# Moving the four PSUM accumulators of the first two output-projection row tiles to the other bank set

## The chip, the cores and the metric

The kernel runs on one NeuronCore of one Trainium2 chip. The metric is the device time of one execution in microseconds (us), given as the median of several runs.

## What is computed

Two independent sequences of 512 rows and 1024 columns pass through a trunk of two layers. Cut to what matters here, one layer is:

```
h      = x @ w_in                                   # attention, HGRN2 and gate inputs
o_att  = window_attention(...)                      # 512 columns
o_hg   = hgrn2_branch(...)                          # 512 columns
mixed  = sigmoid(ga) * (o_att @ w_proj_att) + sigmoid(gb) * (o_hg @ w_proj_hgrn)
x      = layer_norm(ALPHA * x + mixed @ w_out)      # the output projection
x      = layer_norm(ALPHA * x + square(relu(x @ w_ff1)) @ w_ff2)
```

## The kernel before, in words

All values are fp32. Large matmuls are made of three passes: every operand is split into a high part (a cast to fp32r, on ACT) and a low part (the difference, on DVE or POOL), and `high*high + low*high + high*low` is accumulated in PSUM. The 1024 rows of both sequences stand as eight row tiles of 128; `g` is the sequence, `j` the row tile (0 to 7).

PSUM is one pool of two sets of four banks. `mm_ps` (line 109) hands out the four banks tagged `mm` in turn, `sm_ps` (line 112) the four tagged `sm`. An allocation of a set takes the bank that was given out four allocations earlier, and the first matmul into it waits until that bank's last reader is done. The framework sets these waits as semaphores. `mm` serves the projections; `sm` serves the transposes, the attention scores and values, the small products of HGRN2 and part of the second feed-forward matmul.

The stretch around the change, once per layer:

- **Branch projections** (lines 821 to 842). For each of eight column tiles `m_` and both sequences, `project` (line 190) runs 12 matmuls (lines 152 to 154) into an `mm` bank. In the second half of the loop (the attention branch), DVE reads the bank with the gate (line 838), adds the other branch (839), ACT casts the high part of `mixed` (841) and DVE subtracts for the low part (842). Line 838 is the only reader of the bank. The results are the tiles `mx`, 128 columns of `mixed` per step `k`.
- **Weights of the output projection** (`load_rows`, line 844, called in line 864). Eight row blocks `wo[0]` to `wo[7]` of `w_out` are loaded into the three buffers `raw`, cast on ACT (line 131) and subtracted on DVE (even blocks) or POOL (odd blocks) (line 132).
- **Output projection** (lines 871 to 904). `out_proj(j, n, k)` adds step `k` of row tile `j` and column half `n`: three matmuls (lines 879, 880, 881) of 128x512. The first `lead = 2` row tiles are done together with `k` outermost, so that four accumulators are open at once and each `wo[k]` is used for 12 matmuls as it arrives. Row tiles 2 to 7 follow one after the other, 24 matmuls per accumulator. DVE reads each accumulator in line 896 and goes on with the layer norm.
- **Transposes** `x1.put` (line 173). From `j = 4` on, the finished row tiles are transposed on PE into `sm` banks (line 180) and split by ACT (185) and DVE (186) for the first feed-forward matmul.

Each engine works its instructions off in the program's order; loads are issued by SP in the program's order.

Of the kernel before, what the change touches and what calls it, by code (L numbers as in the profile page):

```python
# [87 lines left out]
def tile_encoder_trunk(  # L88
# [20 lines left out]
    def mm_ps():  # L109
        return psum.tile([P, 512], F32, tag="mm", name="mm")  # L110
# [680 lines left out]
    for l in range(DEPTH):  # L791
# [20 lines left out]
        with tc.tile_pool(name=f"ff{l}", bufs=1) as fp:  # L812
# [55 lines left out]
            lead = 2  # L868
            pend = {}

            def out_proj(j, n, k):
                if k == 0:
                    pend[j, n] = mm_ps()
                g, r = divmod(j, 4)
                ts = slice(r * P, (r + 1) * P)
                h = slice(n * 512, (n + 1) * 512)
                mh, ml = mx.at(g, k, 0)[:, ts], mx.at(g, k, 1)[:, ts]
                wh, wl = wo[k][:, 0, h], wo[k][:, 1, h]
                nc.tensor.matmul(pend[j, n], mh, wh, start=(k == 0), stop=False)  # L879
                nc.tensor.matmul(pend[j, n], ml, wh, start=False, stop=False)  # L880
                nc.tensor.matmul(pend[j, n], mh, wl, start=False, stop=(k == KT - 1))  # L881

            for j in range(8):
                y = acc_tile()
                nc.sync.dma_start(y, x_rows(l, j))
                if j == 0:
                    for k in range(KT):
                        for i in range(lead):
                            for n in range(2):
                                out_proj(i, n, k)  # L890
                for n in range(2):
                    h = slice(n * 512, (n + 1) * 512)
                    if j >= lead:
                        for k in range(KT):
                            out_proj(j, n, k)
                    nc.vector.scalar_tensor_tensor(
                        y[:, h], y[:, h], ALPHA, pend.pop((j, n)), op0=ALU.mult, op1=ALU.add
                    )
                layer_norm(y, gb, fp)
                acc.append(y)  # L900
                if j >= 4:
                    x1.put(j - 4, acc[j - 4])
# [210 lines left out]
```

## Time and profile before

| | us |
|---|---|
| median of 3 runs | 3051.74 |
| lowest and highest of them | 3050.33, 3055.02 |
| the profiled execution, its own time | 3051.14 |
| its span in the trace | 3049.3 |
| PE busy | 2950.1 (97% of the span) |
| DVE busy | 1668.9 (55%) |
| ACT busy | 1092.6 (36%) |
| POOL busy | 862.1 (28%) |

The mean granted clock of TensorE is 0.989 of full speed over the span. The output projection of the first layer begins at 750.47 us, that of the second at 2261.03 us of the span. In the timeline, each row is one instruction or a few merged ones: its start, its length, the engine, the line in the kernel, what it writes from what, and in brackets how long the engine sat idle before it and what released it. Matmuls are pipelined, so that the next one starts before the length shown is over; the distance of their starts is what counts.

### The profile page before, as it was taken

The page shows a single profiled execution, that of the slowest core. Times are in us where ns is not written, and L with a number is a line of the kernel's source. Part 1 is how long each engine was busy: PE and PEld are TensorE (multiplying, and loading weights), DVE is VectorE, ACT ScalarE, POOL GpSimd, SP SyncE. Part 2 cuts the span into 40 slices and gives each one's busy share as a digit, 9 for nine tenths or more (in the row PEclk, how much of TensorE's full clock was granted, in tenths as well). Part 3 has the DMA queues.
Part 4 walks back from the last instruction along what each step waited for, and adds up shares of the span by engine and source line. Part 5 has one row for each costly group of instructions (what it writes and reads, how often), then busy time and mean ns, then how long its engine had stood idle before and what let it go on. Part 6 is the DMA issues. An engine that isn't in the chain of part 4 may idle for free.

```text
span 3049.3 us, 42766 instructions
## 1 busy us (share of the span) xinstructions
PE 2950.1 (97%) x16720; PEld 2398.4 (79%) x16720; DVE 1668.9 (55%) x2909; ACT 1092.6 (36%) x1858; POOL 862.1 (28%) x532
## 2 busy tenths in 40 slices
PE   8999999999999999999999999999999999989997
PEld 6777787877888887788777777878878888878886
DVE  5888748126444344445678887570265434344457
ACT  3344447422122222343333444473231222224332
POOL 4221111112222222454542221101131222234544
PEclk9999999999999999999999999999999999999999
DMA  3111222246123446533521112222470243564334
GB/s 127 36 40 39 67 83 68 82 160 212 48 84 132 160 161 244 193 97 111 168 76 36 43 43 70 84 67 98 160 227 6 102 154 138 188 254 159 96 118 146
DMA packets 278379, 348.77 MB, mean 114 GB/s; under 512 B 16033, under 2 KB 184609, under 8 KB 269985
## 3 DMA queue, kind: packets, MB, share of 16 engines
q1 hardware_dynamic: 276880, 342.82, 33.7%
q8 instruction: 132, 2.16, 0.3%
q10 hardware_dynamic: 1296, 3.21, 0.3%
q14 instruction: 71, 0.57, 0.1%
HBM read 238.77 MB, written 100.66 MB: 111 GB/s over the span
## 4 chain that ended last, share of the span: by engine, by line
PE 82%; DVE 11%; DMA 3%; issue 2%; ACT 1%; POOL 1%; SPq 0%; POOLq 0%; ACTq 0%; DVEq 0%
PE mm L152 17%; PE mm L154 16%; PE mm L153 16%; PE mm L978 3%; PE mm L979 3%; PE sm L978 3%; PE sm L979 3%; PE sm L980 3%; PE mm L980 3%; PE mm L879 2%; PE mm L881 2%; PE mm L880 2%; PE sm L709 1%; PE sm L655 1%; PE sm L699 1%
## 5 line engine op out<-in xcount | busy, mean ns | idle before, releaser
L152 PE MATMUL mm<-X,w 128*128 128x512 f32 x2624 | 1033.5, 394 | 3.2 <-ACT w L131 2.8
L153 PE MATMUL mm<-X,w 128*128 128x512 f32 x2624 | 1029.0, 392 | 1.1 <-DVE X L186 1.1
L154 PE MATMUL mm<-X,w 128*128 128x512 f32 x2624 | 1026.8, 391 | 1.0 <-POOL w L132 1.0
L132 POOL TENSOR_TENSOR w<-raw,w 128x1024 fp32r<-128x1024 f32 (+1 forms) x179 | 417.8, 2335 | 1362.9 <-ACT w L131 1238.7
L152 PEld LDWEIGHTS mm<-X,w 128*128 128x128 f32 x2624 | 493.7, 188 | 111.0 <-issue 3.8
L154 PEld LDWEIGHTS mm<-X,w 128*128 128x128 f32 x2624 | 494.1, 188 | 101.9 <-POOL w L132 1.9
L153 PEld LDWEIGHTS mm<-X,w 128*128 128x128 f32 x2624 | 494.1, 188 | 99.6 <-DVE X L186 1.4
L131 ACT CAST w<-raw 128x1024 fp32r<-128x1024 f32 (+1 forms) x330 | 321.2, 975 | 374.9 <-PE sm L980 106.6
L919 DVE TENSOR_TENSOR X<-t 128x512 f32<-128x512 f32 x128 | 88.5, 692 | 390.2 <-ACT t L918 390.2
L132 DVE TENSOR_TENSOR w<-raw,w 128x1024 fp32r<-128x1024 f32 (+1 forms) x153 | 184.4, 1210 | 174.3 <-ACT w L131 174.2
L968 POOL TENSOR_TENSOR raw<-X 128x512 f32<-128x512 f32 x128 | 173.7, 1359 | 227.9 <-DVE w L132 226.2
L918 ACT ACTIVATE t<-mm 128x512 f32<-128x512 f32 x128 | 76.5, 598 | 422.7 <-PE mm L154 422.7
L978 PE MATMUL mm<-w 128*128 128x512 f32 x480 | 190.1, 397 | 25.1 <-ACT w L131 19.3
L979 PE MATMUL mm<-w 128*128 128x512 f32 x480 | 189.6, 395 | 0.6 <-DVE w L132 0.6
L980 PE MATMUL mm<-w 128*128 128x512 f32 x480 | 189.0, 394 | 0.0
L978 PE MATMUL sm<-w 128*128 128x512 f32 x384 | 149.5, 389 | 0.0
L980 PE MATMUL sm<-w 128*128 128x512 f32 x384 | 149.4, 389 | 0.0
L979 PE MATMUL sm<-w 128*128 128x512 f32 x384 | 149.4, 389 | 0.0
L978 PEld LDWEIGHTS mm<-w 128*128 128x128 f32 x480 | 91.3, 191 | 46.6 <-ACT w L131 20.2
L808 DVE TENSOR_TENSOR X<-raw,X 128x512 fp32r<-128x512 f32 x32 | 20.7, 689 | 195.8 <-ACT X L807 195.8
L879 PE MATMUL mm<-X 128*128 128x512 f32 x256 | 102.9, 402 | 11.9 <-DVE t L838 11.9
L966 POOL TENSOR_TENSOR w<-X,w 128x512 fp32r<-128x512 f32 x64 | 85.0, 1329 | 97.6 <-ACT w L962 96.0
(190 smaller groups left out, 3918.1 us busy)
## 6 DMA issues: line engine op xcount, KB each, us to landing
hsp<-X SPq DMA_DIRECT2D x64, 1024.0 KB
raw<-hsp SPq DMA_DIRECT2D x192, 256.0 KB
raw<-in_w_in_dram SPq DMA_DIRECT2D x84, 512.0 KB
raw<-in_w_ff_dram SPq DMA_DIRECT2D x64, 512.0 KB
X<-in_w_ff_dram SPq DMA_DIRECT2D x32, 1024.0 KB
gates<-gt SPq DMA_DIRECT2D x64, 256.0 KB
t<-gates SPq DMA_DIRECT2D x64, 256.0 KB
w<-hsp SPq DMA_DIRECT2D x24, 512.0 KB
```

What stands on the lines that cost most here:

```text
L131: (first or nc.scalar.copy)(hi, src)
L132: (eng or nc.gpsimd).tensor_tensor(lo, src, hi.bitcast(F32), op=ALU.subtract)
L152: nc.tensor.matmul(ps, ah, bh, start=(i == 0), stop=False)
L153: nc.tensor.matmul(ps, ah, bl, start=False, stop=False)
L154: nc.tensor.matmul(ps, al, bh, start=False, stop=(i == n - 1))
L879: nc.tensor.matmul(pend[j, n], mh, wh, start=(k == 0), stop=False)
L919: nc.vector.tensor_tensor(out[g], t, t, op=ALU.mult)
L966: nc.gpsimd.tensor_tensor(w[:, 1, 512:], src, w[:, 0, 512:].bitcast(F32), op=ALU.subtract)
L968: nc.gpsimd.tensor_tensor(raw[:, 512:], block(b0, k), block(b1, k), op=op)
L978: nc.tensor.matmul(ps[r], hh, wh, start=first, stop=False, **kw)
L979: nc.tensor.matmul(ps[r], hh, wl, start=False, stop=False, **kw)
L980: nc.tensor.matmul(ps[r], hl, wh, start=False, stop=stop, **kw)
```

## The change

The four accumulators of the first two row tiles (`j < lead`, both halves `n`) are taken from the `sm` set; those of row tiles 2 to 7 come from `mm` as before. Nothing else differs.

```
 
             def out_proj(j, n, k):
                 if k == 0:
-                    pend[j, n] = mm_ps()
+                    pend[j, n] = (sm_ps if j < lead else mm_ps)()
                 g, r = divmod(j, 4)
```

The order of the instructions is the same on every engine; the tiles that they name and the semaphores that they wait for differ. The following rows stand on PE at the start of the output projection in the first layer, before the change (names with numbers are buffers: `mm_...` is an accumulator, the first `X_...` is `wo[0]`, the second is the high or low part of `mixed`; in brackets the semaphores by the engine or queue that raises them).

```order
L154 MATMUL mm_6912<-X_6225,w_6888 128x512
L879 MATMUL mm_6987<-X_6931,X_6283 128x512 [waits DMAHW4_49,DMAHW3_49,DMAHW5_49,DMAHW2_49,DMAHW6_49,DMAHW1_49,DMAHW7_49,DMAHW0_49,DVE_49]
L880 MATMUL mm_6987<-X_6931,X_6284 128x512
L881 MATMUL mm_6987<-X_6931,X_6283 128x512
L879 MATMUL mm_6991<-X_6931,X_6283 128x512 [waits DVE_49]
L880 MATMUL mm_6991<-X_6931,X_6284 128x512
L881 MATMUL mm_6991<-X_6931,X_6283 128x512
L879 MATMUL mm_6995<-X_6931,X_6283 128x512 [waits DVE_49]
L880 MATMUL mm_6995<-X_6931,X_6284 128x512
L881 MATMUL mm_6995<-X_6931,X_6283 128x512
L879 MATMUL mm_6999<-X_6931,X_6283 128x512 [waits DVE_49]
```

The same rows with the change:

```order
L154 MATMUL mm_6912<-X_6225,w_6888 128x512
L879 MATMUL sm_6987<-X_6931,X_6283 128x512 [waits DMAHW4_49,DMAHW3_49,DMAHW5_49,DMAHW2_49,DMAHW6_49,DMAHW1_49,DMAHW7_49,DMAHW0_49,PE_49]
L880 MATMUL sm_6987<-X_6931,X_6284 128x512
L881 MATMUL sm_6987<-X_6931,X_6283 128x512
L879 MATMUL sm_6991<-X_6931,X_6283 128x512
L880 MATMUL sm_6991<-X_6931,X_6284 128x512
L881 MATMUL sm_6991<-X_6931,X_6283 128x512
L879 MATMUL sm_6995<-X_6931,X_6283 128x512
L880 MATMUL sm_6995<-X_6931,X_6284 128x512
L881 MATMUL sm_6995<-X_6931,X_6283 128x512
L879 MATMUL sm_6999<-X_6931,X_6283 128x512
```

The wait for DVE is gone from all four first matmuls, and the first of them now waits for PE's own semaphore. Also gone is the wait for DVE at the first matmul of each of the next four accumulators (row tiles 2 and 3).

One wait appears that was not written out before, at step `k = 4` of the first accumulator, here with the change (`X_6951` is `wo[4]`; before, the row of line 881 had no brackets):

```order
L879 MATMUL sm_6999<-X_6946,X_6283 128x512
L880 MATMUL sm_6999<-X_6946,X_6284 128x512
L881 MATMUL sm_6999<-X_6946,X_6283 128x512
L879 MATMUL sm_6987<-X_6951,X_6285 128x512 [waits Activation_49]
L880 MATMUL sm_6987<-X_6951,X_6286 128x512
L881 MATMUL sm_6987<-X_6951,X_6285 128x512 [waits DVE_49]
L879 MATMUL sm_6991<-X_6951,X_6285 128x512
```

It is the wait for the low part of `wo[4]`, which DVE makes. Before, the DVE wait of an earlier row already covered it.

## Rows read from the trace of the kernel before

**Rows 1.** The page, part 1: busy time of each engine.

```profile
PE 2950.1 (97%) x16720; PEld 2398.4 (79%) x16720; DVE 1668.9 (55%) x2909; ACT 1092.6 (36%) x1858; POOL 862.1 (28%) x532
```

**Rows 2.** PE's waits: engine, line, for whom; us, times, longest.

```profile
PE mm L879 <- DVE t L838: 11.9, 6, 3.5
```

**Rows 3.** Timeline of PE, end of the projections and start of line 879, first layer.

```profile
727.80 0.39 PE L154 MATMUL mm<-X,w 128*128 128x512 f32 x1
...
750.24 0.39 PE L154 MATMUL mm<-X,w 128*128 128x512 f32 x1
750.47 0.39 PE L879 MATMUL mm<-X 128*128 128x512 f32 x1
...
752.30 0.50 PE L879 MATMUL mm<-X 128*128 128x512 f32 x1 [0.99 <-DVE t L838]
...
755.00 0.50 PE L879 MATMUL mm<-X 128*128 128x512 f32 x1 [1.74 <-DVE t L838]
...
759.48 0.80 PE L879 MATMUL mm<-X 128*128 128x512 f32 x1 [3.52 <-DVE t L838]
...
760.50 0.63 PE L881 MATMUL mm<-X 128*128 128x512 f32 x1
...
762.21 0.63 PE L879 MATMUL mm<-X 128*128 128x512 f32 x1
...
763.87 0.39 PE L879 MATMUL mm<-X 128*128 128x512 f32 x1
```

**Rows 4.** Timeline of PE, the same place in the second layer.

```profile
2261.03 0.39 PE L879 MATMUL mm<-X 128*128 128x512 f32 x1
...
2262.89 0.50 PE L879 MATMUL mm<-X 128*128 128x512 f32 x1 [1.02 <-DVE t L838]
...
2265.59 0.80 PE L879 MATMUL mm<-X 128*128 128x512 f32 x1 [1.74 <-DVE t L838]
...
2266.61 0.63 PE L881 MATMUL mm<-X 128*128 128x512 f32 x1
2270.08 0.80 PE L879 MATMUL mm<-X 128*128 128x512 f32 x1 [2.85 <-DVE t L838]
...
2275.16 0.39 PE L879 MATMUL mm<-X 128*128 128x512 f32 x1
```

**Rows 5.** Timeline of DVE in the same stretch, first layer.

```profile
751.56 0.68 DVE L838 TENSOR_TENSOR t<-mm,t 128x512 f32<-128x512 f32 x1
...
754.26 0.68 DVE L838 TENSOR_TENSOR t<-mm,t 128x512 f32<-128x512 f32 x1
754.86 1.22 DVE L132 TENSOR_TENSOR X<-raw,X 128x1024 fp32r<-128x1024 f32 x1
...
758.75 0.68 DVE L838 TENSOR_TENSOR t<-mm,t 128x512 f32<-128x512 f32 x1
759.35 1.21 DVE L132 TENSOR_TENSOR X<-raw,X 128x1024 fp32r<-128x1024 f32 x1
...
779.06 1.37 DVE L896 SCALAR_TENSOR_TENSOR acc<-acc,mm 128x512 f32<-128x512 f32 x2 [15.92 <-PE mm L881]
```

**Rows 6.** Windows around the waits: us, busy us (x instructions) by engine; PEclk, DMA share, GB/s.

```profile
750.40:763.00 12.60, 6.34 (x20) 4.17 (x19) 10.65 (x12) 5.79 (x8) 2.69 (x1) 0.73 0.94 309
...
2261.00:2275.00 14.00, 8.40 (x22) 5.56 (x21) 10.79 (x12) 6.16 (x8) 3.66 (x2) 0.63 0.96 298
```

**Rows 7.** Tile `sm` from 600 to 830 us, matmuls: ns min/median/max, first and last start.

```profile
L180 PE MATMUL sm<-ident,acc x16: 270/272/273, 813.5 to 826.1; 128*128 128x128 f32 x16
```

**Rows 8.** Timeline of POOL: the low part of `wo[7]`, first and second layer.

```profile
763.44 2.40 POOL L132 TENSOR_TENSOR X<-raw,X 128x1024 fp32r<-128x1024 f32 x1 [5.16 <-ACT X L131]
...
2274.03 2.39 POOL L132 TENSOR_TENSOR X<-raw,X 128x1024 fp32r<-128x1024 f32 x1 [5.16 <-ACT X L131]
```

**Rows 9.** The chain that ended last: the spilled-hidden read after the first feed-forward matmul.

```profile
1214.82 10.59 DMA raw<-hsp
...
2726.22 7.88 DMA raw<-hsp
```

More of the change, by code (lines that the diff above doesn't have):

```diff
@@ L872, in out_proj @@
                 if k == 0:
-                    pend[j, n] = mm_ps()
+                    pend[j, n] = (sm_ps if j < lead else mm_ps)()
                 g, r = divmod(j, 4)
```

## The prediction
> **What bounds the kernel now.** I read the page's busy times first: PE works for 97% of the span [rows 1], so a change pays only if it closes a gap on PE, or makes PE's instructions run quicker. Next came the list of PE's waits. Line 879, the first matmul of an accumulator, waits 11.9 us in all, in six pieces, and always for DVE's line 838 [rows 2]. That is the gate multiply that reads the bank of a branch projection.
>
> The timeline of PE shows where the six pieces lie: three at the start of each layer's output projection [rows 3, 4]. Since a wait for several things is put down to one of them, I checked the name against DVE's own timeline. Line 838 ends at 751.56 + 0.68 = 752.24, 754.26 + 0.68 = 754.94 and 758.75 + 0.68 = 759.43 us [rows 5]; PE starts again at 752.30, 755.00 and 759.48 [rows 3]. Each restart follows its release by about 0.06 us, so the bank really is what was missing. DVE comes late because between the gate multiplies it also makes the low parts of `wo` [rows 5]; PE has finished the projections by 750.47 and meets DVE's arrears.
>
> **What the waits cost.** The idle figures alone understate it, so I count start to start. Undisturbed, PE needs (750.24 - 727.80) / 99 = 0.2267 us per matmul (99 steps lie between these two rows) [rows 3]. In the first layer the matmul at 763.87 is the 22nd of the output projection, 21 steps after the one at 750.47. Undisturbed it would start at 750.47 + 21 x 0.2267 = 755.23, so 8.64 us are lost. In the second layer the 22nd starts at 2275.16 and would start at 2261.03 + 4.76 = 2265.79: 9.37 us are lost [rows 4]. Together 18.01 us.
>
> This splits in two. The holes themselves are the idle time in brackets plus what pipelining would have saved, 0.39 - 0.23 = 0.16 us each (0.63 - 0.23 = 0.40 for the last one of the second layer, which follows a 0.63 us matmul): 0.99 + 1.74 + 3.52 + 0.48 = 6.73 and 1.02 + 1.74 + 2.85 + 0.72 = 6.33 us, 13.1 together [rows 3, 4]. The other 4.9 us are slow matmuls. From 760.50 to 762.21, four steps take 0.427 us each, nearly twice the normal step [rows 3]; the granted clock over the two stretches is 0.73 and 0.63 on average [rows 6]. That is a mixture of the two levels, 2.4 and 1.2 GHz: after its holes PE runs at the lower one for a while.
>
> The Trainium skill, "TensorE: Matmul & The Clock Gate", section "A second HAM failure mode: psum-queue depth-cycling", describes this pattern: small PE pauses between matmul groups as banks cycle cost throughput beyond the pause, through repeated loss of the clock. The trace agrees, with 4.9 us beyond 13.1. By a reading that counts the holes alone the saving would be 13.1 us and the time 3038.1. The same page, "What's actually happening", holds that the number of matmuls at the low clock varies from run to run, which speaks against taking the 4.9 us as fixed; no single trace can show that.
>
> I bound the clock part from rows. At least it is nothing, a saving of 13.1. At most all 18 steps from the 4th matmul to the 22nd run at 0.427, in both layers: 2 x 18 x 0.20 = 7.2 us, a saving of 20.3. I take the measured 4.9, as it belongs to the execution whose time I start from.
>
> **The change, part by part.**
> - *The four accumulators move to `sm`.* Between 600 and 813.5 us nothing touches an `sm` bank [rows 7], so these are free, and the three holes per layer go. The gain is 18.0 us, on PE's path.
> - *The new wait on PE's own semaphore* at the first matmul is for the last earlier write into that bank, over 150 us ago [rows 7]. I take 0; if PE had to empty its pipeline once, it would be one matmul length, 0.4 us per layer [rows 3].
> - *The waits at row tiles 2 and 3 go.* PE then reaches row tile 2 at 750.47 + 96 x 0.2267 = 772.2 us; the last gate multiply frees its bank at 759.43 [rows 5]. Cost 0, with 12.8 us in hand.
> - *What is late next.* PE now arrives earlier at steps 4 to 7 (12 matmuls or 2.72 us each): 761.35, 764.1, 766.8 and 769.5 us. The low part of `wo[4]`, whose wait is now written out, is ready at 754.86 + 1.22 = 756.1, that of `wo[6]` at 759.35 + 1.21 = 760.6 [rows 5]. The last operand is the low part of `wo[7]` on POOL, ready at 763.44 + 2.40 = 765.84 [rows 8], which leaves 3.7 us. In the second layer step 7 starts at 2261.03 + 84 x 0.2267 = 2280.07 and POOL is done at 2276.42 [rows 8], again 3.7 us. None of these depends on when PE starts the output projection. Cost 0, but this is the thinnest cover: gone, it costs what exceeds 3.7 us, plus some low clock.
> - *The readers.* Line 896 now empties `sm` banks. DVE sits idle for 15.92 us before the first of them [rows 5], so it takes them 8.64 us earlier, at about 770.4. The transposes that want the `sm` banks next move from 813.5 to about 805 [rows 7], 30 us later. Cost 0.
> - *The number of allocations* in each set changes by four per layer, which is a whole turn of four banks, so later tiles meet the same banks as before. Cost 0.
>
> From here to the end everything is released by PE's progress, so the shift should reach the end. Sum: 3051.14 - 18.0 = 3033.1 us, against the profiled execution's own time, 0.6 us below the median of the three runs. I predict 3033.
>
> **The rivals.**
> 1. *The wait moves to the last operands.* If the weights of step 7 come later than in this trace, part of the stall returns. For it: in the stretch the DMA engines are 0.94 and 0.96 busy [rows 6], and the `wo[7]` load is among this work. Against it: 3.7 us in hand in both layers, and no transfer moves. A load 7 us later gives back some 3.5 us of waiting and 2 of clock per layer, 11 us in all: 3044. I price this case at 3039 to 3045.
> 2. *It doesn't do what it says*, or the gain is lost later: 3045.6 to 3057. Another release might sit right behind the bank. Against it: the DVE wait is the only one in the rows of the second to fourth accumulator, it is gone after the change, and the first matmul never stalled on its many other waits (0.23 us after the projection) [rows 3].
> 3. *Slower, at the turn to the second feed-forward matmul.* PE waits there for a read of spilled hidden values, which took 10.59 us in one layer and 7.88 in the other for the same bytes [rows 9]. If the 9 us earlier arrival met heavier traffic, this leg could grow. It decides the sign once both together grow by over 18 us, from 18.5 to above 36.5; for 0.2% slower they must grow by 24: 3057 and more. For it: the 2.7 us spread. Against it: all transfers there are released by PE's progress, so the traffic shifts along.
>
> **How the numbers follow.** About 0.2% (6.1 us) is what a measurement of this kernel can tell from no change; so faster means below 3045.6. My forecast, the holes gone and nothing late after, covers 3051.14 - 20.3 = 3030.8 to 3038.1, and a little to both sides for scatter between runs: chance 0.82. Rival 1 has 0.10, rival 2 0.05, rival 3 0.03. Faster is 0.82 + 0.10 = 0.92, same 0.05, slower 0.03. The range runs from 3029.4 (the low bound less 1.4, the distance of the lowest run from the median) into rival 1, to 3041.
>
> **What would show it.** In the profile after, line 879 should have lost its waits for line 838; the 22nd matmul of each output projection should start 4.76 us after the first; the granted clock of these stretches should be 1.00; and line 896 should come 8 to 9 us earlier after the end of the projections. A wait of lines 879 to 881 for POOL or ACT line 131/132 would show rival 1. A longer hidden read would show rival 3. I am wrong if PE still stops at the first four accumulators, or if the saving at row tile 2 doesn't reach the end of the span.

## The result and the profile after

| | us |
|---|---|
| before, first comparison, median of 4 runs | 3052.85 |
| with the change, median of 4 runs | 3031.75 (3029.97 to 3035.61) |
| ratio | 0.9936, 95% interval 0.9924 to 0.9949 |
| with the change, repeated beside 11 runs of before | 3035.27, ratio 0.9951, 0.9938 to 0.9963 |
| predicted | 3033 (3029.4 to 3041) |

The kernel became faster by 0.5 to 0.6%. Applied to the kernel before's 3050.5 us (median of those 11 runs), the two ratios are savings of 19.5 and 14.9 us; 18.0 were forecast. (The ratios are the recorded estimates. The quotients of the medians are 0.9931 and 0.9950, that is 21.1 and 15.2 us.)

PE's waits with the change (engine and line, for whom; us in all, times, longest), the longest and all those of the second feed-forward matmul:

```profile
PE sm L262 <- DVE t2k L259: 18.2, 9, 2.7
PE mm L978 <- ACT w L131: 16.7, 2, 8.4
...
PE mm L978 <- DMA w<-hsp: 6.3, 6, 2.6
...
PE mm L979 <- DVE w L132: 1.0, 1, 1.0
```

Line 879, which waited 11.9 us for line 838 [rows 2], is not in the list any more. The timeline of PE at the output projection of the first layer, its 1st, its 22nd and its 97th matmul (the first of row tile 2):

```profile
749.02 0.39 PE L879 MATMUL sm<-X 128*128 128x512 f32 x1
...
753.78 0.39 PE L879 MATMUL sm<-X 128*128 128x512 f32 x1
...
770.78 0.39 PE L879 MATMUL mm<-X 128*128 128x512 f32 x1
```

The 22nd comes 4.76 us after the 1st, as computed for an undisturbed stream; before, it took 13.40 us [rows 3]. In the second layer, where it took 14.13 us [rows 4], it is 4.76 us as well (2247.96 and 2252.72). The 97th follows after 21.76 us in both layers, which is 96 x 0.2267: no new wait has come in. The windows over the same stretches:

```profile
750.40:763.00 12.60, 12.60 (x57) 10.46 (x56) 10.11 (x11) 5.77 (x7) 2.97 (x2) 1.00 0.90 295
...
2252.00:2266.00 14.00, 14.00 (x63) 11.58 (x63) 7.99 (x8) 5.30 (x7) 7.18 (x3) 1.00 0.94 293
```

PE is busy throughout, at a granted clock of 1.00, where it was 0.73 and 0.63 [rows 6]. Behind it, DVE empties the first accumulators, and POOL finishes `wo[7]`:

```profile
768.94 1.37 DVE L896 SCALAR_TENSOR_TENSOR acc<-acc,sm 128x512 f32<-128x512 f32 x2 [7.03 <-PE sm L881]
```

```profile
762.77 2.40 POOL L132 TENSOR_TENSOR X<-raw,X 128x1024 fp32r<-128x1024 f32 x1 [5.72 <-ACT X L131]
```

Line 896 starts 19.92 us after the first matmul of the output projection, where it took 28.59 [rows 3, 5]: 8.67 us earlier. POOL is done at 765.17; step 7 starts at 749.02 + 84 x 0.2267 = 768.06, so 2.9 us were left of the cover that I had put at 3.7. In the second layer it was 3.3 us, and in the repeated profile of the change 3.4 and 2.4.

### The profile page after: what moved, and what is told of

It reads as the page before. It is cut to its first block, busy times and chain, and to the rows that moved or that the text cites. A ratio compares the mean times of both kernels' runs of the same rounds, so it can differ in the third digit from the quotient of the medians.

```text
span 3028.2 us, 42766 instructions
## 1 busy us (share of the span) xinstructions
PE 2943.1 (97%) x16720; PEld 2393.4 (79%) x16720; DVE 1668.6 (55%) x2909; ACT 1092.6 (36%) x1858; POOL 861.4 (28%) x532
## 4 chain that ended last, share of the span: by engine, by line
PE 85%; DVE 8%; DMA 3%; issue 2%; ACT 1%; POOL 1%; SPq 0%; POOLq 0%; ACTq 0%; DVEq 0%
PE mm L152 18%; PE mm L154 17%; PE mm L153 17%; PE mm L978 3%; PE mm L979 3%; PE mm L980 3%; PE sm L979 3%; PE sm L980 3%; PE sm L978 3%; PE mm L881 1%; PE mm L880 1%; PE mm L879 1%; PE sm L709 1%; PE sm L655 1%; PE sm L699 1%
## 5 line engine op out<-in xcount | busy, mean ns | idle before, releaser
L978 PE MATMUL mm<-w 128*128 128x512 f32 x480 | 190.0, 397 | 23.1 <-ACT w L131 16.7
L225 ACT ACTIVATE gt<-mm 128x512 f32<-128x512 f32 x64 | 38.3, 599 | 197.9 <-PE mm L154 142.4
```

The source lines that it names most:

```text
L978: nc.tensor.matmul(ps[r], hh, wh, start=first, stop=False, **kw)
```

## The experiments

**The kernel before, profiled again.** No edit.

> The kernel before, profiled a second time, to see what scatters by itself. If the three holes at each output projection are set by when line 838 frees the banks, they come again with the same lengths to within 0.1 us (about 1.0, 1.7 and 3.5 us in the first layer; 1.0, 1.7 and 2.9 in the second). The number of slow matmuls behind them may differ. If the hole at the turn to the second feed-forward matmul is chance (11.0 and 8.4 us of idle time before, 8.3 and 8.4 with the change), it lies anywhere between 8 and 11 here too. If it is a gain of the change, it stays at 11 in the first layer.

```profile
PE mm L978 <- ACT w L131: 17.9, 2, 9.5
PE mm L879 <- DVE t L838: 11.7, 6, 3.5
```

The holes came again, at 1.01, 1.74 and 2.85 us in the first layer and 0.90, 1.74 and 3.51 in the second. The last one varies by up to 0.7 us, more than expected. It is the shorter one where the matmuls ahead of it, behind the second hole, already ran at the low clock (0.79 us long here in the first layer, 0.51 in the second), so that PE came later to its bank:

```profile
753.67 0.79 PE L879 MATMUL mm<-X 128*128 128x512 f32 x1 [1.74 <-DVE t L838]
...
2266.24 0.51 PE L879 MATMUL mm<-X 128*128 128x512 f32 x1 [1.74 <-DVE t L838]
```

From the 1st to the 22nd matmul 9.52 and 9.20 us were lost, 18.7 in all beside 18.0 in the first profile. The hole at the turn of the first layer (line 978, at the start of the second feed-forward matmul) was 9.5 us, between the 11.0 and the 8.3 of the two profiles compared. The first profile of before has it so:

```profile
PE mm L978 <- ACT w L131: 19.3, 2, 11.0
```

**The change, repeated.** No edit.

> The change again, for its size and for a second profile. From the predicted steps alone: 18.0 us less than the kernel before, ratio 0.9941. No wait of line 879 for line 838. If the 3 us by which the first measurement went beyond the sum are chance, the ratio comes nearer to 0.994, and the turn's hole in the first layer scatters between 8 and 11 us; if the earlier arrival shortens that hole, the ratio is 0.993 and the hole is 8.3 again.

The ratio is 0.9951 (0.9938 to 0.9963), the turn's hole in the first layer 9.4 us, the stretch again free of holes and 4.76 us long in both layers. The two ratios lie on either side of 0.9941, which the sum gave.

**One layer at a time.** The edit of the first run; the second has `l == 1` in its place.

```
-                    pend[j, n] = mm_ps()
+                    pend[j, n] = (sm_ps if j < lead and l == 0 else mm_ps)()
```

> The sm banks in the first layer alone. If each layer's holes are local: 8.6 us less than before, ratio 0.9972, with the holes of the second layer in place (1.0, 1.7, 2.9 us). If the shift also shortens the turn of the first layer: 11.3 less, 0.9963. If only the second layer counted: no difference.

> The sm banks in the second layer alone. If each layer's holes are local: 9.4 us less than before, ratio 0.9969, with the holes of the first layer in place (1.0, 1.7, 3.5 us). The two single layers should add up to the whole change. If the gain of the whole comes in part from the first layer's turn, the two together fall short of it by about 3 us only when that turn's hole is 11 us here.

Ratios 0.9972 (0.9961 to 0.9984) and 0.9967 (0.9955 to 0.9980): 8.5 and 10.1 us. They add up to 18.6. The untouched layer kept its holes, 5.5 us of idle time in each run, 0.94, 1.74 and 2.84 us in both, where 3.5 had been expected for the last one of the first layer (this row stands in both lists of waits):

```profile
PE mm L879 <- DVE t L838: 5.5, 3, 2.8
```

The turn of the first layer held 9.6 us of idle time in the run with the first layer changed and 9.3 in the other. So that hole takes no notice of the shift.

**Only the second row tile.**

```
-                    pend[j, n] = mm_ps()
+                    pend[j, n] = (sm_ps if j == 1 else mm_ps)()
```

> Only the two accumulators of the second row tile come from sm. If each hole belongs to its own bank, the second and third hole go and the first stays (1.0 us of idle time, 1.15 with pipelining, in each layer): 18.0 - 2.3 = 15.7 us less than before, ratio 0.9949, with the clock at full rate. If PE must sit out DVE's arrears whatever the bank, the first hole grows to the whole arrears and nothing is gained, ratio 1.000.

Ratio 0.9948 (0.9934 to 0.9961), as the first theory has it. One hole is left at each place, that of the second accumulator, which is still on `mm` (the first is too, but its bank was free in time):

```profile
748.36 0.39 PE L879 MATMUL mm<-X 128*128 128x512 f32 x1
...
750.44 0.50 PE L879 MATMUL mm<-X 128*128 128x512 f32 x1 [1.24 <-DVE t L838]
...
754.65 0.39 PE L879 MATMUL sm<-X 128*128 128x512 f32 x1
```

```profile
745.00:775.00 30.00, 28.76 (x127) 23.53 (x126) 19.34 (x27) 11.64 (x14) 14.51 (x6) 1.00 0.81 249
```

From the 1st to the 22nd it takes 6.29 us, 1.5 more than undisturbed (in the second layer, with a hole of 0.97 us, 1.3 more), and the clock stays at 1.00. PE need not sit out DVE's arrears; each hole belongs to its bank.

**Only the fourth accumulator.**

```
-                    pend[j, n] = mm_ps()
+                    pend[j, n] = (sm_ps if (j, n) == (1, 1) else mm_ps)()
```

> Only the fourth accumulator comes from sm. If each hole belongs to its own bank, the third hole goes (3.7 and 3.2 us with pipelining) and the first two stay (1.0 and 1.7 us idle). The gain beyond 6.9 us is what the slow matmuls behind the third hole cost: 6.9 us less than before if the clock falls after the second hole all the same, 11.8 if it no longer falls; ratio 0.9977 to 0.9961. If PE must sit out the arrears whatever the bank, nothing is gained.

Ratio 0.9977 (0.9969 to 0.9986), the low end of what was expected. The timeline and the window of the first layer:

```profile
751.06 0.50 PE L879 MATMUL mm<-X 128*128 128x512 f32 x1 [1.25 <-DVE t L838]
...
753.76 0.79 PE L879 MATMUL mm<-X 128*128 128x512 f32 x1 [1.74 <-DVE t L838]
...
755.21 0.63 PE L879 MATMUL sm<-X 128*128 128x512 f32 x1
...
759.90 0.44 PE L881 MATMUL mm<-X 128*128 128x512 f32 x1
760.18 0.39 PE L879 MATMUL sm<-X 128*128 128x512 f32 x1
```

```profile
745.00:775.00 30.00, 27.01 (x106) 21.42 (x105) 14.75 (x17) 11.58 (x14) 14.76 (x6) 0.89 0.84 256
```

The third hole, the longest, is gone, and the clock falls all the same after the second. Eleven steps from 755.21 to 759.90 take 0.426 us each. Over both layers the 22nd matmul is still 6.44 + 6.25 = 12.7 us late; the holes make 6.6 of that and the slow matmuls 6.1, more than the 4.9 in the kernel before. So the stretches became shorter by 5.3 us in these profiles, no more than the third holes themselves (6.9): nothing of the clock's price was saved, since the low clock stayed. Rows 4 had hinted at this: in the second layer of the kernel before, the matmuls right behind the second hole are already 0.80 and 0.63 us long, before the third hole begins.

**One row tile in the lead.** The change with less work before the last weights are needed.

```
-            lead = 2
+            lead = 1
```

> The change with one row tile in the lead instead of two, so that PE arrives at step 7 after 42 matmuls instead of 84, at about 760.0 instead of 769.5 us. This takes away the cover of the last weights. If their readiness was read rightly (765.84 us at POOL), PE waits for the low part of wo[7], some 5.8 us in each layer in up to four pieces, plus 0 to 3.6 us of low clock: 12 to 19 us more than the change, so no better than the kernel before by over 6 us (ratio to before 0.998 to 1.000). If the cover was larger than read, the time is that of the change, ratio 0.994.

Ratio to before 1.0003 (0.9994 to 1.0012): against the repeated change's 0.9951 this is 0.52%, or 16 us, inside the 12 to 19. The whole gain is gone. The last two waits of the first layer, at step 7, for the high and the low part of `wo[7]`, and the 55th matmul:

```profile
762.87 0.49 PE L879 MATMUL sm<-X 128*128 128x512 f32 x1 [1.60 <-ACT X L131]
...
765.30 0.80 PE L881 MATMUL sm<-X 128*128 128x512 f32 x1 [1.70 <-POOL X L132]
...
769.16 0.39 PE L879 MATMUL mm<-X 128*128 128x512 f32 x1
```

With 0.53 and 0.64 us before them, for the low parts of `wo[5]` and `wo[6]`, they make four holes; behind the last of them matmuls are slow again. The 55th matmul, at 769.16, would start undisturbed at 749.80 + 54 x 0.2267 = 762.04, so 7.1 us are lost in this layer, and 8.0 in the second. This is the wait of rival 1, brought about by PE's earlier arrival instead of a later load, and it shows that the second row tile in the lead is the cover of the last weights, `wo[5]` to `wo[7]`.

**The early blocks of `w_ff2` behind the reads.** The change, and the loads at the turn in another order.

```
-            for b, c in early:
-                load_block(*b, c, a_tile)
             ahead = 2
...
                 feed(i + ahead)
+                if ph == 0 and k >= 2 and early:
+                    b, c = early.pop(0)
+                    load_block(*b, c, a_tile)
```

> The change, and the four last early blocks of w_ff2 are loaded inside the loop of the second feed-forward matmul from its third step on, behind the reads of hidden values, instead of ahead of it. It tells what the hole at the turn hangs on. If the read of hidden values is late because it stands in SP's queue behind these blocks (issued at 1214.82, after four loads that wait for free slots), the hole of 8 to 11 us per layer shrinks to under 3 and the time falls by 10 to 18 us below the change, ratio to before 0.988 to 0.991. If the read is slow by itself, the hole stays, ratio 0.994. If the blocks then come too late for step 8, a new wait of line 978 appears and the time is that of the change or up to 20 us more.

Ratio to before 0.9890 (0.9877 to 0.9904), 3017.14 us beside 3050.55, and so faster than both kernels of this case. SP's queue at the turn of the first layer, with the change alone and then with this edit:

```profile
1199.30 0.34 SPq L934 DMA_DIRECT2D hsp<-X  x1
1199.69 4.37 SPq L941 DMA_DIRECT2D X<-in_w_ff_dram  x3
1204.15 1.70 SPq L958 DMA_DIRECT2D raw<-hsp  x3
```

```profile
1197.25 0.34 SPq L934 DMA_DIRECT2D hsp<-X  x1
1197.68 1.04 SPq L958 DMA_DIRECT2D raw<-hsp  x1
```

The read of hidden values no longer stands behind three loads that hold the queue for 4.37 us, and its transfer is shorter too. The chain of waits has it at 8.52 us with the change alone and at 5.66 here:

```profile
1204.15 8.52 DMA raw<-hsp
```

```profile
1197.68 5.66 DMA raw<-hsp
```

PE's waits at this place, over both layers, went from 16.7 us in two holes to small ones:

```profile
PE mm L978 <- ACT w L131: 2.8, 3, 1.0
```

The rows take the first layer's gain apart. From the issue of the last spill (line 934) to the landing of the read it is 1204.15 + 8.52 - 1199.30 = 13.37 us with the change alone and 1197.68 + 5.66 - 1197.25 = 6.09 here: 7.3 us less, 4.4 of it in the queue and 2.9 in the transfer. The hole fell by as much, from 8.33 to 1.04 us. Why the transfer is shorter was not tested.

## Why the prediction was right

- **What was missing was the bank.** Shown. With the banks moved the three holes per layer vanish; with half of them moved, just those vanish. That the release by line 838 and PE's restart lay 0.06 us apart was a sound reading.
- **Why DVE is late.** Only in part as predicted. The low parts of `wo` are not what lies between the gate multiplies at 751.56 and 754.26 us [rows 5]: there DVE only runs lines 838, 839 and 842, and waits 0.68 us for ACT's line 841. Before the last gate multiply, the one behind the longest hole, stand one low part of 1.22 us and line 839, which took 2.83 us, where it took 0.68 at 761.09. It met a low part that POOL made:

```profile
755.59 2.69 POOL L132 TENSOR_TENSOR X<-raw,X 128x1024 fp32r<-128x1024 f32 x1 [6.48 <-ACT X L131]
```

```profile
755.99 2.83 DVE L839 TENSOR_TENSOR acc<-acc,t 128x512 f32<-128x512 f32 x1
```

  Its end, 758.82, lies 0.54 us behind POOL's, 758.28. No run moved POOL's work, so this cause is argued from the rows and not tested. The sum of the prediction did not hang on it.
- **The size, 18.0 us.** Right for the stretch itself: 13.40 and 14.13 us became 4.76 and 4.76, in both profiles of the change. The measured 19.5 and 14.9 us scatter around it, and the two single layers add up to 18.6.
- **The clock as a term of its own.** Right, and needed: by the holes alone, 13.1 us, the ratio would be 0.9957, which the first interval excludes and the second does not. The traces settle it: the stretches became 18.0 us shorter, not 13.1. The 4.9 us for slow matmuls is one draw. In the first layer it was 1.9 us in the first profile of the kernel before, and 3.2 in the second (9.52 less holes of 6.32). The Trainium skill, "TensorE: Matmul & The Clock Gate", "What's actually happening", says of the matmuls at the low clock at a kernel's start that their number differs from run to run. These traces show the same behind holes in mid-kernel, with 1.9 beside 3.2 us.
- **Terms put at nothing.** The wait on PE's own semaphore, the readers, the transposes and the whole turn of the bank sets cost nothing that the traces show: the 97th matmul comes exactly in step, and the first transpose 54.41 us after the first matmul, where it took 63.07.
- **The cover of the last weights.** Named as the thinnest, at 3.7 us; it was 2.4 to 3.4 with the change, and one row tile less in the lead used it up. Rival 1 was real and did not happen.
- **Rival 2**, no effect, falls with the result.
- **Rival 3**, the turn. It did not grow. The read in the first layer took 10.59 us before [rows 9], 8.94 in the second profile of before, and 8.52 and 8.90 in the two profiles of the change; that in the second layer 7.88, 7.87, 7.88 and 7.88.
- **What went beyond the sum.** The first pair of profiles differs by 21.1 us in span. 18.0 of it is the two stretches. In the changed profile the output projection already begins 1.45 us earlier (749.02 beside 750.47 [rows 3]), before anything was changed, and the first layer's hole at the turn was 11.0 beside 8.3 us. The repeats show both as scatter: that start lies between 746.83 and 751.67 us in the other profiles without the edit at the turn, and that hole between 9.0 and 10.0. Some 1.3 us were lost again after the second layer's output projection: at the turn the lead is still 22.44 us (2735.29 beside 2712.85), and behind it lines 978 and 979 wait six times, 4.6 us in all, where they waited four times, 3.7 us. That is most of it.

## What to carry to other kernels

When two uses of PSUM follow each other and the reader of the first lags, give the second use banks whose last reader was done long ago; the accumulators then hide the lag, as long as their own operands come in time. Price such a wait start to start, from the first to the first undisturbed matmul, since the slow clock behind the holes added 4.9 us to 13.1 here. Then ask what is late next and by how much it is covered: here 2.4 to 3.4 us, which half the work in the lead would not have had.

## What the runs showed of the hardware

The granted clock does not go by the length of one hole. Behind a second hole of 1.74 us the matmuls were quick in the first layer of the first profile of before [rows 3] and slow in its second layer [rows 4]. Nor does it go by the holes alone: with a first hole of 0.99 us they were quick there, with one of 0.94 us slow in both runs with one layer changed. A hole of 1.24 us that stayed by itself left the clock at 1.00. Holes of 1.25 and 1.74 us with three matmuls between them were followed, in both layers, by a stretch at half speed (0.426 us a step), which cost about as much as the one in the kernel before with its third hole of 2.85 to 3.5 us (6.1 beside 4.9 and 5.8 us over both layers). I had expected the longest hole to carry most of the clock's price.

DVE's lines 839 and 842, which read and write SBUF alone, mostly take 0.68 or 0.69 us. All six that took longer between 719 and 759 us in the first profile of before, 1.08 to 2.83 us, met one of POOL's low parts (line 132) and ended 0.54 to 0.56 us behind it. Line 838, which reads a PSUM bank, kept its 0.68 us beside POOL (at 746.77 us).
